# Weight sums by score rows, another order of rooms behind attention, and 640-key rows as 384+256

## The chip, the cores and the metric

The kernel runs on one core of a Trainium2 chip. The metric is device time in microseconds (us) of one launch, as the median of several runs. All numbers of a profile come from one profiled execution.

## The reference

One layer of an encoder on 1024 tokens of width 1024, in float32. It has two token mixers side by side (a causal pooling mixer and a stick-breaking attention of 8 heads), gated and merged, and then a squared-ReLU MLP.

```python
h    = rmsnorm(x, g_pre_mix)
proj = h @ w_in                                   # [u_pool | q | k | v]
y_pool = multiscale_pool(u_pool, ...) @ w_br_pool
# attention, per head, query blocks of 128, causal:
z    = (q @ k.T) * 0.125
attn = sigmoid(z_ts) * prod_{s<j<t} (1 - sigmoid(z_tj)),  s < t
y_sb = (attn @ v) @ w_br_sb
gates  = sigmoid(h @ w_gate + b_gate)             # 2 x 1024 channels
merged = gates[:, :1024] * y_pool + gates[:, 1024:] * y_sb
x = x + rmsnorm(merged @ w_out, g_post_mix)
h2 = rmsnorm(x, g_pre_mlp)
x = x + rmsnorm(square(relu(h2 @ w_up)) @ w_down, g_post_mlp)
```

## The kernel before

Activations lie with channels on the 128 partitions and tokens along the free axis, in two halves of 512 tokens. Every large product is computed from float32 values split into a rounded high part and a low rest (`hi`, `lo`), with three matmuls for one: hi by hi, hi by lo, lo by hi (`mm3`, lines 113 to 117). A product of one 128-row output tile with one half takes 8 steps of 3 matmuls of 512 columns.

The order of instructions on each engine's queue comes from a planner, which simulates the program and issues what it holds ready first; `issue_after(i)` makes what stands in its block follow `i` on the same engine.

**Attention.** For each of the 8 heads, `att_scores` runs over 8 score rows, `i` = 7 down to 0; row `i` holds 128 queries and their (i + 1) x 128 keys. PE computes the scores `z` in pieces of at most 512 keys, from the last key backwards (lines 560 and 563: `q` holds high parts over low rests, so two matmuls are enough). A piece shorter than 256 keys is multiplied at 256 columns. ACT makes `F` and `T` (sigmoids of -z and z, lines 564 and 565), POOL sets the masked part of the last 128 keys of `T` to zero with an affine select (line 567), DVE multiplies `F` up by a scan (line 573) and into `T` (line 577). `att_steps` transposes rows of four (`at`, line 590), ACT and DVE split them into `ahi` and `alo` (598, 599), and PE multiplies them with `v` into `o` (line 615). The sums of `o` go to `oT` (624, 626).

Between these matmuls `pump` puts steps of other products (fillers): later q, k and v, and the gates. A gate's half (`job_gate`) ends with a product on DVE (line 519, tile `gs`), a sigmoid on ACT (520) and a store to DRAM, issued by POOL (521, `gscr`). A change of ACT's table follows the last sigmoid (779).

**Weight sums.** The MLP's down product uses sums of blocks of `w_down`, which are made in DRAM by DMAs alone: `weight_sums` is a generator of 32 DMAs of 1 MB, all issued by POOL (lines 1056 and 1058, destination `wscr`). Sixteen are plain copies and sixteen add to what lies there. The last eight make `s4`: four copies of `s2`, then four additions. They are first read in the down product, far behind attention. Before the change, each store of a gate's half is followed by one.

**Branch products** (`phase_post`). With attention done, ACT and DVE split `oT` into `oh` and `ol` (lines 732 and 733), four tiles each. For every output tile `e` of 8 and both branches `b`, PE computes two halves of 12 matmuls (the pooling branch reads `yh` and `yl`, the attention branch `oh` and `ol`), POOL loads the gate (752), DVE multiplies gate and product (`t`, 756), adds the branches (763) and splits the sum (765), with ACT (764). The first pooling products (`first_pool`) are issued ahead of `phase_post`, and the planner puts those of the second output tile beside them. The products rotate over seven PSUM banks, five of the pool `ps` and two of `dps`.

The tiles of `phase_post` lie in the pool `post`. It takes the room of attention's pools: the tiles `v`, the row tiles `T` and `F` with `ahi` and `alo`, and the small tiles `gs` and `ou`. Each tile waits for the last users of the room it gets (`reuse_waits="tile"`); places are given out in the order in which tags are first asked for. In the same way `ps` takes the banks of attention's `o`, `z` and `at`.

Then follow the output product (`d` from `mg`, first the half h = 0, then h = 1), a chain of norms beside it, and the MLP.

Of the kernel before, what the change touches and what calls it, by code (L numbers as in the profile page):

```python
# [32 lines left out]
P = 128  # L33
# [19 lines left out]
class Block:  # L53
# [460 lines left out]
    def job_gate(self, i, h):  # L514
        nc = self.nc
        d = self.dps.tile([P, H], F32, name="dg", tag="d")
        yield from self.dense_steps(d, self.weights(("g", i)), self.hT[h])
        s = self.sp.tile([P, H], F32, name="gs", tag="gs", bufs=2)
        nc.vector.tensor_mul(s, d, self.rb[h])
        self.after = nc.scalar.activation(s, s, AF.Sigmoid, bias=self.vt[:, V_BG + i : V_BG + i + 1])  # L520
        out = nc.gpsimd.dma_start(self.gscr[i][:, h * H : h * H + H], s)
        with self.tc.issue_after(out.ins):
            next(self.wsums)

    def fillers(self, h):

# [13 lines left out]
    def att_scores(self, h, i):  # L540

        nc = self.nc
        p, j = h // 2, h % 2
        q, qs, k = self.qk[("q", p)][j], self.qk[("qs", p)][j], self.qk[("k", p)][j]
        w = (i + 1) * P
        tl = self.tp.tile([P, w], F32, name="T", tag=f"T{i}", bufs=1)  # L550
        f = self.tp.tile([P, 1024], F32, name="F", tag="F", bufs=1)
        tt = slice(i * P, i * P + P)
        past = self.past[:, 1024 - w :]
        for c in range((w - 1) // H * H, -1, -H):
            n = min(H, w - c)
            top = c + n == w
            cols = slice(c, c + max(256, n))
            z = self.zps.tile([P, H], F32, name="z", tag="z", bufs=3)
            zz = z[:, : max(256, n)]
            m = nc.tensor.matmul(zz, q[:, tt], k[:, cols], start=True, stop=False)  # L560
            if top:
                self.marks.append(m)
            nc.tensor.matmul(zz, qs[:, tt], k[:, cols], start=False, stop=True)  # L563
            nc.scalar.activation(f[:, c : c + n], z[:, :n], AF.Sigmoid, scale=-1.0)  # L564
            nc.scalar.activation(tl[:, c : c + n], z[:, :n], AF.Sigmoid)
            if top:
                nc.gpsimd.affine_select(  # L567
                    out=tl[:, w - P : w], in_=tl[:, w - P : w], pattern=[[-1, P]], compare_op=ALU.is_gt, fill=0.0,
                    base=0, channel_multiplier=1,
                )  # L570

            fr = f[:, c : c + n][:, ::-1]
            nc.vector.tensor_tensor_scan(  # L573
                fr, fr, past[:, c : c + n][:, ::-1], 1.0 if top else f[:, c + n : c + n + 1], ALU.mult, ALU.max
            )
            e = c + n - top
            nc.vector.tensor_mul(tl[:, c:e], tl[:, c:e], f[:, c + 1 : e + 1])  # L577
        return tl
# [66 lines left out]
    def phase_attention(self):  # L645
        tc, nc = self.tc, self.nc
        self.oT = [self.op.tile([P, 1024], F32, name=f"oT{p}", tag=f"oT{p}") for p in range(4)]
        kw = dict(side="right", reuse_waits="tile")
        self.tp = tc.alloc_tile_pool(name="att", bufs=1, **kw)
        self.sp = tc.alloc_tile_pool(name="att_s", bufs=1, **kw)  # L650
        self.credit, self.queue = 0.0, []
        self.w_out = 2.3
        self.pending = None
        self.pin = True
        self.cut = 512
        out = None
        for h in range(8):
            while self.queue:
                self.advance()
            fl = self.fillers(h)  # L660
            n = sum(f[1] for f in fl)
            self.queue = fl
            share = [WS[i] for i in ROWS] if h else [0.0] * 4 + [WS[i] for i in ROWS[4:]]
            w_in = max(0.0, n - (8 if h == 0 else 12) * self.w_out) / sum(share)
            vg = self.job_v(0) if h == 0 else None
            a = {}
            for n_row, i in enumerate(ROWS):
                if n_row == 4:
                    out = self.att_steps(h, 1, [a[r] for r in range(4, 8)])
                a[i] = self.att_scores(h, i)  # L670
                self.pump(w_in * share[n_row])
                if h == 0 and n_row < 4:
                    if n_row == 0:
                        vq = [(vg, 32)] + [(f[0], f[1]) for f in self.fillers(-1)]
                    left = 12 if n_row < 3 else 999
                    while vq and left:
                        left -= 1
                        if next(vq[0][0], self) is self:
                            vq.pop(0)
                if out is not None:  # L680
                    for _ in range(2 if n_row > 3 else 1):
                        next(out, None)
            out = self.att_steps(h, 0, [a[r] for r in range(4)])
        while self.queue:
            self.advance()
        self.queue = self.fillers(8)
        self.w_out = 3.0
        for _ in out:
            pass
        self.pump(self.w_out)  # L690
        self.att_products()
        while self.queue:
            self.advance()
        self.pin = False
        self.cut = 1024
        self.yy = []
        for i in range(8):
            t = self.qp.tile([P, 1024], F32R, name=f"y{'hl'[i % 2]}{i // 2}", tag=("q", "qs", "k")[i % 3], bufs=3)
            nc.gpsimd.dma_start(t.bitcast(F32), self.yscr[i // 2][i % 2].bitcast(F32))
            self.yy.append(t)  # L700
        self.first_pool = [self.dps.tile([P, H], F32, name="dbr", tag="d") for _ in range(2)]
        for h in range(2):
            self.branch_mm(self.first_pool[h], 0, 0, h, (self.yy[0::2], self.yy[1::2]))
        for p in (self.sp, self.tp, self.vp, self.zps):
            p.release()
# [17 lines left out]
    def phase_post(self):  # L723
        tc, nc = self.tc, self.nc
        pp = tc.alloc_tile_pool(name="post", bufs=1, side="right", reuse_waits="tile")
        self.ps = tc.alloc_tile_pool(name="ps", bufs=5, space=PSUM, reuse_waits="tile")
        self.banks = 1
        oh, ol = [], []
        for p in range(4):
            oh.append(pp.tile([P, 1024], F32R, name=f"oh{p}"))  # L730
            ol.append(pp.tile([P, 1024], F32R, name=f"ol{p}"))
            nc.scalar.copy(oh[p], self.oT[p])
            nc.vector.tensor_sub(ol[p], self.oT[p], oh[p].bitcast(F32))
        mg = []
        for h in range(2):
            hi = self.big.tile([P, NK, H], F32R, name=f"mg_hi{h}", tag=f"big_hi{h}")
# [4 lines left out]
        def products(e, b):  # L741
            ds = []
            for h in range(2):
                d = self.bank()
                self.branch_mm(d, e, b, h, xs[b])
                ds.append(d)
            return ds

        def gated(e, b, ds):
            i = 8 * b + e  # L750
            gt = pp.tile([P, 1024], F32, name="gate", tag="gate", bufs=3)
            nc.gpsimd.dma_start(gt, self.gscr[i])
            out = []
            for h in range(2):
                t = pp.tile([P, H], F32, name="t", tag=f"t{b}", bufs=2)
                nc.vector.tensor_mul(t, gt[:, h * H : h * H + H], ds[h])
                out.append(t)
            return out

# [8 lines left out]
        for e in range(8):  # L768
            d0 = nxt
            if e == 0:  # L770
                nxt = products(1, 0)
            p = gated(e, 0, d0)
            d1 = products(e, 1)
            q = gated(e, 1, d1)
            merge(e, p, q)
            if 0 < e < 7:
                nxt = products(e + 1, 0)
        with tc.issue_after(self.after.ins):
            self.table_inst = nc.scalar.preload_act_table_set(TABLES).ins
        pp.release()  # L780
# [9 lines left out]
        for h in range(2):  # L790
# [4 lines left out]
            def mix_out(e, d, first):  # L795
                nc.scalar.copy(mix[e // 4][:, e % 4, :], d)
                sq = acc if first else ch.tile([P, H], F32, name="sq", tag="nf", bufs=2)
                nc.scalar.activation(sq, d, AF.Square)
                if not first:
                    nc.vector.tensor_add(acc, acc, sq)  # L800
# [3 lines left out]
            for e in order:  # L804
                d = self.bank()
                wt = self.weights(("out", 0 if e > 2 else h, e))
                for k, _ in enumerate(self.dense_steps(d, wt, mg[h])):
                    if k == 3 and prev is not None:
                        mix_out(*prev, prev[0] == order[0])
                prev = (e, d)  # L810
            mix_out(*prev, False)
            self.finish_side()
# [550 lines left out]
```

## Time and profile before

| | |
|---|---|
| median of 3 runs | 1279.74 us (1278.86 to 1281.45) |
| profiled execution | 1278.63 us, its span 1276.9 us |
| granted clock of PE | 0.999 |
| PE busy | 1265.7 us, 6035 matmuls |
| DVE busy | 925.7 us |
| ACT busy | 611.0 us |
| POOL busy | 172.1 us |
| DMA | 233.70 MB, of it 88.49 MB on POOL's queue |

PE, PEld (weight loads), DVE, ACT and POOL are engines; SP issues DMAs. In a group's row stand the line, the engine, the operation, the tiles as out<-in, the shapes and the count; after the first bar the busy time in us and the mean duration of one in ns; after the second the idle time of the engine just before these instructions and what ended it. A wait's row has who waited, `<-`, whom for; then us in total, times, the longest. A row of a timeline or of the chain of waits begins with the start in us from the start of the span and the duration in us. "issue" is time in which an engine waited for nothing that the profile shows. In the windows view, the last three columns are PE's granted clock, the busy share of the 16 DMA engines and GB/s.

### The profile page before, as it was taken

To read this page: it belongs to the slowest core of one execution; us is meant where nothing else is said; L and a number is where in the kernel's file an instruction comes from. 1 tells how busy PE (TensorE), PEld (TensorE's weight loads), DVE (VectorE), ACT (ScalarE), POOL (GpSimd) and SP (SyncE) were. 2 spreads that over 40 slices of the span, in tenths; PEclk is the share of its full clock that TensorE was granted. 3 is DMA by queue.
4 is the path that set the end of the run, shared out by engine and by line. 5 is a ranking of instruction groups with operands and counts; after the bars stand their busy time and mean duration, and the time that the engine had idled before them with its cause. 6 is when DMAs were issued, how large, how long until landed. Compare 5 with 4: busy or idle time off the path is not lost.

```text
span 1276.9 us, 16588 instructions
## 1 busy us (share of the span) xinstructions
PE 1265.7 (99%) x6035; PEld 1056.1 (83%) x6035; DVE 925.7 (72%) x1317; ACT 611.0 (48%) x1012; POOL 172.1 (13%) x314
## 2 busy tenths in 40 slices
PE   9999999999999999999999999999999999999997
PEld 6898888889888887888878888888888888888887
DVE  8787688787878737551777979877785655776975
ACT  8235455555555533132456646455454433344452
POOL 1002213211213230000101002211120000001000
PEclk9999999999999999999999999999999999999999
DMA  6254637742757997451529578655569546547651
GB/s 226 66 165 153 210 90 181 147 106 53 185 157 197 248 229 234 142 195 33 179 79 307 181 245 283 216 191 205 177 238 345 194 153 224 191 176 242 200 212 66
DMA packets 75745, 233.70 MB, mean 183 GB/s; under 512 B 8624, under 2 KB 11184, under 8 KB 73488
## 3 DMA queue, kind: packets, MB, share of 16 engines
q1 hardware_dynamic: 47936, 143.64, 34.4%
q0 software_dynamic: 27152, 88.49, 23.1%
q8 instruction: 47, 0.77, 0.2%
q10 hardware_dynamic: 576, 0.52, 0.1%
q14 instruction: 34, 0.28, 0.1%
HBM read 178.10 MB, written 83.89 MB: 205 GB/s over the span
## 4 chain that ended last, share of the span: by engine, by line
PE 91%; DVE 4%; issue 2%; ACT 1%; DMA 1%; POOL 0%; SPq 0%; DVEq 0%; ACTq 0%; POOLq 0%
PE d L116 20%; PE d L117 20%; PE d L115 20%; PE dg L117 4%; PE dg L116 4%; PE dg L113 4%; PE o L615 3%; PE at L590 2%; PE dqk L116 2%; PE dqk L117 2%; PE dqk L113 1%; PE z L563 1%; PE z L560 1%; PE du L116 1%; PE zu L116 1%
## 5 line engine op out<-in xcount | busy, mean ns | idle before, releaser
L116 PE MATMUL d<-blo,whi 128*128 128x512 f32 (+1 forms) x456 | 172.3, 378 | 0.0
L117 PE MATMUL d<-bhi,wlo 128*128 128x512 f32 (+1 forms) x456 | 171.9, 378 | 0.0
L115 PE MATMUL d<-bhi,whi 128*128 128x512 f32 (+1 forms) x456 | 168.7, 378 | 0.0
L573 DVE TENSOR_TENSOR_SCAN F<-F,past 128x512 f32<-128x512 f32 (+3 forms) x96 | 94.0, 979 | 22.4 <-ACT F L564 21.0
L85 ACT CAST whi<-wraw 128x512 fp32r<-128x512 f32 (+1 forms) x88 | 67.7, 800 | 72.4 <-PE d L116 35.0
L113 PE MATMUL dg<-hT_hi,whi 128*128 128x512 f32 x253 | 101.8, 402 | 0.0
L117 PE MATMUL dg<-hT_hi,wlo 128*128 128x512 f32 x256 | 100.8, 394 | 0.0
L116 PE MATMUL dg<-hT_lo,whi 128*128 128x512 f32 x256 | 100.4, 392 | 0.0
L86 DVE TENSOR_TENSOR wlo<-wraw,whi 128x512 fp32r<-128x512 f32 (+1 forms) x88 | 77.6, 904 | 30.1 <-ACT whi L85 30.0
L116 PEld LDWEIGHTS d<-blo,whi 128*128 128x128 f32 x456 | 85.7, 188 | 16.1
L117 PEld LDWEIGHTS d<-bhi,wlo 128*128 128x128 f32 x456 | 85.8, 188 | 15.9
L115 PEld LDWEIGHTS d<-bhi,whi 128*128 128x128 f32 x456 | 85.5, 188 | 15.8
L564 ACT ACTIVATE F<-z 128x512 f32<-128x512 f32 (+3 forms) x96 | 47.2, 493 | 61.6 <-DVE T L577 37.0
L116 PE MATMUL d<-b_lo,whi 128*128 128x512 f32 x196 | 76.2, 390 | 0.4 <-DVE b_lo L825 0.4
L115 PE MATMUL d<-b_hi,whi 128*128 128x512 f32 x196 | 75.6, 389 | 0.0
L117 PE MATMUL d<-b_hi,wlo 128*128 128x512 f32 x196 | 74.7, 389 | 0.0
L1112 DVE TENSOR_TENSOR wlo<-slots_hi,whi 128x1024 fp32r<-128x1024 f32 x29 | 35.5, 1225 | 52.3 <-ACT whi L1110 52.3
L599 DVE TENSOR_TENSOR alo<-at,ahi 128x512 fp32r<-128x512 f32 (+1 forms) x96 | 51.9, 553 | 24.8 <-ACT ahi L598 23.6
L1110 ACT CAST whi<-slots_hi 128x1024 fp32r<-128x1024 f32 x29 | 30.5, 1051 | 81.1 <-PE d L116 65.2
L598 ACT CAST ahi<-at 128x512 fp32r<-128x512 f32 (+1 forms) x96 | 45.1, 481 | 45.2 <-PE at L590 42.0
L1110 ACT CAST whi<-slots_lo 128x1024 fp32r<-128x1024 f32 x27 | 28.4, 1053 | 74.0 <-PE d L116 60.3
L577 DVE TENSOR_TENSOR T<-T,F 128x255 f32<-128x255 f32 (+4 forms) x96 | 52.8, 556 | 12.1 <-POOL T L567 4.2
(319 smaller groups left out, 3310.1 us busy)
## 6 DMA issues: line engine op xcount, KB each, us to landing
wraw<-w SPq DMA_DIRECT2D x80, 512.0 KB, 4.3
wscr<-w POOLq DMA_DIRECT2D x24, 1024.0 KB, 10.3
ext_b<-ascr SPq DMA_DIRECT2D x40, 512.0 KB, 4.3
gscr<-gs POOLq DMA_DIRECT2D x32, 256.0 KB, 4.8
gate<-gscr POOLq DMA_DIRECT2D x16, 512.0 KB, 3.7
pscr<-p SPq DMA_DIRECT2D x32, 256.0 KB, 3.2
braw<-w SPq DMA_DIRECT2D x16, 512.0 KB, 5.5
ascr<-c POOLq DMA_DIRECT2D x32, 256.0 KB, 4.7
```

Of the source, the lines that this page charges most:

```text
L85: nc.scalar.copy(hi[:, c], raw[:, c])
L86: self.last_lo = nc.vector.tensor_sub(lo[:, c], raw[:, c], hi[:, c].bitcast(F32)).ins
L113: nc.tensor.matmul(ps, wh, rh, start=first and i == 0, stop=False)
L115: nc.tensor.matmul(ps, wh, rh, start=first and i == 0, stop=False)
L116: nc.tensor.matmul(ps, wh, rl, start=False, stop=False)
L117: nc.tensor.matmul(ps, wl, rh, start=False, stop=last and i == n - 1)
L564: nc.scalar.activation(f[:, c : c + n], z[:, :n], AF.Sigmoid, scale=-1.0)
L573: nc.vector.tensor_tensor_scan(fr, fr, past[:, c : c + n][:, ::-1], 1.0 if top else f[:, c + n : c + n + 1], ALU.mult, ALU.max)
L577: nc.vector.tensor_mul(tl[:, c:e], tl[:, c:e], f[:, c + 1 : e + 1])
L598: nc.scalar.copy(hi[:, c:], at[:, c:])
L599: nc.vector.tensor_sub(lo[:, c:], at[:, c:], hi[:, c:].bitcast(F32))
L1110: last_split[0] = nc.scalar.copy(hi, src).ins
```

## The change

Six edits:

1. `job_gate` no longer issues a weight sum behind its store.
2. In attention a weight sum is issued on POOL behind the affine select of the score rows number 1, 3 and 6 of each head (rows `i` = 6, 4 and 1): 24 sums. Four more follow the merges of output tiles 1, 3, 5 and 7 in the branch products, and four the output tiles 1, 3, 5 and 7 of the output product's first half.
3. A row's keys are cut in two as 512 below and the rest above, but so that the upper piece has at least 256. Only rows of 640 keys change: 384 below and 256 above in place of 512 and 128.
4. In the pool `post`, the place of the tag `t0` (two tiles of 128x512, 4 KB a partition) is asked for first, ahead of `oh0`.
5. In the pool `ps`, the place of `ms` is asked for first, ahead of the product banks.
6. The products `t` of gate and branch are issued on DVE behind the last `ol`.

```diff
@@ job_gate
-        out = nc.gpsimd.dma_start(self.gscr[i][:, h * H : h * H + H], s)
-        with self.tc.issue_after(out.ins):
-            next(self.wsums)
+        nc.gpsimd.dma_start(self.gscr[i][:, h * H : h * H + H], s)
@@ att_scores
-        for c in range((w - 1) // H * H, -1, -H):
-            n = min(H, w - c)
-            top = c + n == w
+        low = min(H, w - 2 * P) if w > H else 0
+        for c, n in ((low, w - low), (0, low)):
+            if n == 0:
+                continue
+            top = c == low
...
-                nc.gpsimd.affine_select(
+                self.masked = nc.gpsimd.affine_select(
@@ phase_attention
                 self.pump(w_in * share[n_row])
+                if n_row in (1, 3, 6):
+                    with tc.issue_after(self.masked.ins):
+                        next(self.wsums)
@@ phase_post
         self.banks = 1
+        pp.tile([P, H], F32, name="t", tag="t0", bufs=2)
+        self.ps.tile([P, H], F32, name="ms", tag="ms", bufs=1)
...
-            nc.vector.tensor_sub(ol[p], self.oT[p], oh[p].bitcast(F32))
+            ol_done = nc.vector.tensor_sub(ol[p], self.oT[p], oh[p].bitcast(F32)).ins
...
-                nc.vector.tensor_mul(t, gt[:, h * H : h * H + H], ds[h])
+                with tc.issue_after(ol_done):
+                    nc.vector.tensor_mul(t, gt[:, h * H : h * H + H], ds[h])
...
             if 0 < e < 7:
                 nxt = products(e + 1, 0)
+            if e % 2:
+                next(self.wsums)
...
                     if k == 3 and prev is not None:
                         mix_out(*prev, prev[0] == order[0])
+                if h == 0 and e % 2:
+                    next(self.wsums)
```

## The prediction

> **What bounds the kernel now.** I read the page first, then the waits of PE, then the stretches in which PE waits.
>
> ```profile
> PE 1265.7 (99%) x6035; PEld 1056.1 (83%) x6035; DVE 925.7 (72%) x1317; ACT 611.0 (48%) x1012; POOL 172.1 (13%) x314
> ...
> PE 91%; DVE 4%; issue 2%; ACT 1%; DMA 1%; POOL 0%; SPq 0%; DVEq 0%; ACTq 0%; POOLq 0%
> ```
>
> The kernel is a row of matmuls: PE is busy for 99% of the span and carries 91% of the chain that ended last. So only two things can move the time: fewer columns through PE, or fewer places where PE stands. The longest waits of PE inside attention and the branch products are these:
>
> ```profile
> PE d L116 <- DVE ol L733: 0.8, 1, 0.8
> ...
> PE dg L115 <- DVE v L509: 0.4, 1, 0.4
> PE d L115 <- ACT oh L732: 0.3, 1, 0.3
> ```
>
> Those on `ol` and `oh` are one place, the change from attention to the branch products. The timeline of PE shows it (start, duration, instruction):
>
> ```profile
> 483.65 0.39 PE L117 MATMUL d<-yh,wlo 128*128 128x512 f32 x1
> 484.34 0.50 PE L115 MATMUL d<-oh,whi 128*128 128x512 f32 x1 [0.30 <-ACT oh L732]
> 485.60 0.50 PE L116 MATMUL d<-ol,whi 128*128 128x512 f32 x1 [0.76 <-DVE ol L733]
> 485.94 0.39 PE L117 MATMUL d<-oh,wlo 128*128 128x512 f32 x1
> ```
>
> Matmuls overlap, so a wait is read from start to start and not from the idle in brackets. Undisturbed, 12 matmuls of 512 columns take 2.72 us from start to start, 0.227 each:
>
> ```profile
> 518.15 0.39 PE L115 MATMUL d<-yh,whi 128*128 128x512 f32 x1
> ...
> 520.87 0.39 PE L115 MATMUL d<-yh,whi 128*128 128x512 f32 x1
> ```
>
> The three steps here are 0.69, 1.26 and 0.34 us, together 2.29 where 0.68 would do. The place costs 1.6 us. The chain that ended last, over the same place, says why:
>
> ```profile
> 474.94 1.01 DMA gscr<-gs
> 475.95 7.29 issue
> ```
>
> ACT itself is free at 475.95, as its timeline says (474.67 + 1.28), and copies `oh` only at 483.24:
>
> ```profile
> 474.67 1.28 ACT L779 ACT_TABLE_LOAD   x1
> 483.24 3.89 ACT L732 CAST oh<-oT 128x1024 fp32r<-128x1024 f32 x4 [7.29 <-issue]
> ```
>
> The step before, in the chain, is the last gate's store, and its landing is in the DMA view of 474.9 to 475.2 (size, us from issue to landing):
>
> ```profile
> gscr<-gs POOLq DMA_DIRECT2D x1, 256.0 KB, 7.9
> ```
>
> 474.94 + 7.9 = 482.8, then `oh` starts. `oh0` is the first tile of the pool `post`, so this row says that the first place of that pool lies in the room of `gs`, which is free only when the store has read it. The store is slow because POOL's queue and the DMA engines are full: POOL's timeline, and the window of 455 to 490 (the last columns are clock, DMA share, GB/s).
>
> ```profile
> 469.67 1.23 POOL L1056 DMA_DIRECT2D wscr<-w  x1
> 474.94 0.57 POOL L521 DMA_DIRECT2D gscr<-gs  x1 [4.05 <-ACT gs L520]
> 475.93 1.18 POOL L1056 DMA_DIRECT2D wscr<-w  x1 [0.42 <-issue]
> 476.58 2.14 POOL L752 DMA_DIRECT2D gate<-gscr  x3
> ```
>
> ```profile
> 455.00:490.00 35.00, 33.94 (x157) 27.79 (x156) 13.19 (x18) 12.43 (x18) 8.82 (x13) 1.00 1.04 243
> ```
>
> A weight sum stands on either side of the store, and the DMA engines are busy for the whole stretch (1.04).
>
> **Part 1, rows of 640 keys, 384+256 in place of 512+128.** Before, the last 128 keys are multiplied at 256 columns all the same. PE's timeline, the 512 pair of one such row and the next instruction:
>
> ```profile
> 425.81 0.40 PE L560 MATMUL z<-k,q 128*128 128x512 f32 x1
> 426.05 0.40 PE L563 MATMUL z<-k,qs 128*128 128x512 f32 x1
> 426.29 0.40 PE L113 MATMUL dg<-hT_hi,whi 128*128 128x512 f32 x1
> ```
>
> The 256 pair stays and the 512 pair becomes a 384 pair; the kernel has 384 pairs already, in its rows of 896 keys. The other lengths split as before. By groups (after the bar: busy us, mean ns, idle before):
>
> ```profile
> L560 PE MATMUL z<-k,q 128*128 128x512 f32 x48 | 19.2, 399 | 0.0
> ...
> L560 PE MATMUL z<-k,q 128*128 128x384 f32 x16 | 5.5, 342 | 0.0
> ```
>
> 57 ns less for each of 16 matmuls (two a head, 8 heads) is 0.9 us. As a bound, the 512 pair above takes 0.48 from start to start and a pair of 384 this:
>
> ```profile
> 436.48 0.33 PE L560 MATMUL z<-k,q 128*128 128x384 f32 x1
> 436.65 0.34 PE L563 MATMUL z<-k,qs 128*128 128x384 f32 x1
> 436.82 0.40 PE L113 MATMUL dg<-hT_hi,whi 128*128 128x512 f32 x1
> ```
>
> 0.34, so at most 0.14 x 8 = 1.1 us. The lower end is 0.7: where PE waits on DVE, a shorter matmul is eaten by the wait, and one or two heads could lie so. I take 0.9, since PE hardly waits in attention. The sigmoids, scans and products of ACT and DVE touch the same 640 elements in the same number of instructions: nothing.
>
> **Part 2, rooms and order at the branch products.** The first place of `post` goes to `t0`, so `oh0` moves on to a room of attention's row tiles, whose last readers are transposes of the score rows. `oh` can then start when ACT is free, at 475.95 at the latest: `oh0` is done at 477.0 and `ol0` (1.24 on DVE) at 478.3; all four `ol` are done by about 482. PE asks for them from 483.88 on (483.65 + 0.23), so the cover is 5.6 us, and the 1.6 us go. Late next is the gated product: `t` now waits for the gate's store and, by the new order, stands behind the last `ol` on DVE. Behind `t` on DVE wait the merges and the low halves of the next branch weights; PE needs `t` to get a bank back. Before, the first `t` ran here, ended by the landing of the gate load:
>
> ```profile
> 489.42 1.29 DVE L756 TENSOR_TENSOR t<-gate,dbr 128x512 f32<-128x512 f32 x2 [0.47 <-DMA gate<-gscr]
> ```
>
> Seven banks rotate. Two hold the first products, two those of the second output tile, and the products with `oh` start at 483.88; after three halves of 2.72 us all seven are in use, and PE needs the first one back at 492.0. The first `t` is done at 490.1 even if the gate lands as late as now. Cover 1.9 us at worst, more with no sum ahead of the gates. The room held for `ms` moves the product banks to places freed earlier; PE waits for no bank now: nothing. If the cover of `t` were gone, the 1.6 would come back in part; so this term lies between -1.6 and 0, and I take -1.6.
>
> **Part 3, the 32 weight sums.** They are the same DMAs with the same issue cost; 24 now stand behind the masks of rows 6, 4 and 1 of each head, 4 among the branch products, 4 in the first half of the output product. POOL is busy 13% of the span. PE waits for no DMA now, so taking sums from the end of attention gains nothing but what part 2 has counted, and adding them later costs nothing while weights and gates land in time. SP's weight loads share the engines with them: none now comes into the full stretch, and four into the one behind it, where the thirteen gate loads below land in 3.6 us. I take 0, with the ends in the rivals.
>
> **Sum.** -0.9 - 1.6 = -2.5 us. The profiled execution takes 1278.63 us, 1.73 of it outside the span, and becomes 1276.1. It lies 1.1 below the median of the three runs, so on their scale 1279.74 - 2.5 = 1277.2. That is 0.2% of 1279.74 (2.56 us), about what a measurement of this kernel can tell from no change; the forecast sits on that line.
>
> **Rivals.** *One, the place keeps a wait* (the rooms fall otherwise and `oh` still stands on the store, or `t` takes over). For it: the room of `oh0` is only inferred from a wait. Against it: the cover worked out above. Only the columns are left, 1279.7 - 0.9 = 1278.8.
>
> *Two, attention's own two waits go as well,* as the planner lays the work out anew. The longer is the `dg` row above, 0.4 us idle. At `ol` 0.76 idle cost 1.26 - 0.23 = 1.03 from start to start, so 0.4 is about 0.6, and with a smaller wait on `alo` about 1.0, an estimate. For it: DVE's and POOL's queues are ordered anew. Against it: the first waits at the very start of attention, before any sum and any row of 640 keys was issued. 1277.2 - 1.0 = 1276.2.
>
> *Three, slower: the sums hold up the masks.* A sum ahead of a mask in POOL's queue, and DVE just after:
>
> ```profile
> 236.58 1.23 POOL L1056 DMA_DIRECT2D wscr<-w  x1
> 237.26 0.87 POOL L567 TENSOR_SCALAR_AFFINE_SELECT T<-T 128x128 f32<-128x128 f32 x1
> ```
>
> ```profile
> 238.16 0.69 DVE L577 TENSOR_TENSOR T<-T,F 128x511 f32<-128x511 f32 x1 [0.55 <-POOL T L567]
> ```
>
> Behind each of the 24 sums wait the next row's mask, the zero fills of `ahi`/`alo` and the gate stores. At 0.55 us each, passed on to PE, that is 13.2 us and 1290.4. Against it: as many sums stand in that queue now, PE did not wait here, and a sum right behind a mask has the longest time to the next one. It decides from 10 of the 24 on (5.5 us, more than 2.5 + 2.56).
>
> *Four, slower: sums hold up the gate loads.* Both are issued by POOL. Three gates behind a sum landed late, the other thirteen did not (two DMA views, 476.5 to 477.7 and 490 to 548):
>
> ```profile
> gate<-gscr POOLq DMA_DIRECT2D x3, 512.0 KB, 13.5
> ```
>
> ```profile
> gate<-gscr POOLq DMA_DIRECT2D x13, 512.0 KB, 3.6
> ```
>
> A gate is asked for well ahead: this one is for products that PE begins at 518.15 and ends, first half, at 520.87.
>
> ```profile
> 508.45 0.53 POOL L752 DMA_DIRECT2D gate<-gscr  x1 [4.49 <-DVE t L756]
> ```
>
> That is 12.4 us of lead; 13.5 would be 1.1 late, and the bank of that half is needed again only six halves later (16 us). So it decides from a landing of about 28 us, twice the worst seen; four gates late by 1.5 us beyond that would make 1279.7 - 2.5 + 6 = 1283. [...]
>
> **How the numbers follow.** Forecast (both gains) 0.63, own range 1276.2 to 1278.2 for the ends of part 1 and the scatter of a median; rival one 0.15, two 0.10, three 0.08, four 0.04. The forecast lies on the line, so half of it counts as faster (0.32) and half as within 0.2% (0.31). Faster: 0.32 + 0.10 = 0.42. Within: 0.31 + 0.15, and 0.03 of rival three where few sums count, 0.49. Slower: 0.09. The range 1275.0 to 1280.0 holds the forecast and rivals one and two with the runs' scatter of about 1 us; three and four lie above it.
>
> **What the changed profile would show.** Part 1: `z` at 512 columns x40 and at 384 x24. Part 2: no wait of PE on `oh` or `ol`; `oh` of ACT near 476 or earlier, no 7 us before it; `t` after the last `ol`. Part 3: sums at even distances, DMA share of the last 20 us of attention well under 1.0, gates landing in 4 to 14 us without a wait of PE. The prediction is wrong if PE waits on `t`, a gate or a weight in the branch products, if masks hold DVE long enough for a new wait of PE on `alo` or `v`, or if `oh` still stands on a store.

## The result, and the profile after

The changed kernel takes 1303.92 us (median of 5 runs, 1302.48 to 1305.09) against 1279.74 us before: 1.0188 times as long, 95% interval 1.0177 to 1.0200. The forecast was 1277.2 us with a range up to 1280.0; it was wrong, on the side of rival three. The profiled execution takes 1302.48 us with a span of 1300.8 us, 23.9 us more than the span before.

The page's line of engines, and its chain that ended last:

```profile
PE 1272.1 (98%) x6035; PEld 1060.7 (82%) x6035; DVE 925.2 (71%) x1317; ACT 609.7 (47%) x1012; POOL 167.9 (13%) x314
...
PE 86%; DMA 4%; DVE 4%; issue 4%; ACT 1%; POOL 1%; SPq 0%; DVEq 0%; POOLq 0%; ACTq 0%
PE d L116 20%; PE d L117 20%; PE d L115 20%; PE dg L117 3%; PE dg L116 3%; PE dg L113 3%; DMA wscr<-w 3%; PE o L616 2%; PE dqk L116 2%; PE dqk L117 2%; PE at L591 2%; PE dqk L113 1%; PE z L564 1%; PE z L561 1%; DVE F L574 1%
```

PE stands for 1300.8 - 1272.1 = 28.7 us where it stood 11.2 before: +17.5. It is also busy for 6.4 us more, with the same 6035 matmuls. Together that is the 23.9. And a weight sum (`wscr<-w`) has come into the chain.

Where it lies is read from two starts, of the first `dbr` (in an answer on that tile: shortest, median and longest in ns, first and last start) and of the first product with `mg`. Before:

```profile
L115 PE MATMUL dbr<-yh,whi x8: 389/389/389, 473.0 to 480.3; 128*128 128x512 f32 x8
```

```profile
561.67 0.39 PE L115 MATMUL d<-mg_hi,whi 128*128 128x512 f32 x1
```

After:

```profile
L115 PE MATMUL dbr<-yh,whi x8: 389/389/389, 498.5 to 505.8; 128*128 128x512 f32 x8
```

```profile
585.54 0.39 PE L115 MATMUL d<-mg_hi,whi 128*128 128x512 f32 x1
```

Attention ends 25.5 us later. The branch products take 87.0 us where they took 88.7, which is 1.6 us less. From `mg` on nothing changes: 1300.8 - 585.5 is 215.3 and 1276.9 - 561.7 is 215.2. So all of the loss lies in attention, and the waits of PE in its last hundred us name it:

```profile
PE o L616 <- POOL ahi L597: 11.8, 2, 8.7
PE o L616 <- ACT ahi L599: 4.2, 2, 3.8
PE o L616 <- DVE alo L600: 1.9, 1, 1.9
```

Line 597 is a zero fill of `ahi` on POOL, some 0.2 us of work. What POOL itself waited for in that stretch:

```profile
POOL wscr L1070 <- DMA wscr<-w: 38.1, 4, 11.4
POOL wscr L1068 <- DMA wscr<-wscr: 16.2, 3, 6.5
```

Line 1070 issues a copy and line 1068 an addition. POOL stood 54 us in front of weight sums, each time for the landing of another sum. POOL's timeline shows the last case (issue or work, and in brackets the idle time ahead of it):

```profile
463.55 1.72 POOL L1068 DMA_DIRECT2D wscr<-w  x1
466.25 0.61 POOL L521 DMA_DIRECT2D gscr<-gs  x1 [0.98 <-ACT gs L520]
...
468.07 0.30 POOL L568 TENSOR_SCALAR_AFFINE_SELECT T<-T 128x128 f32<-128x128 f32 x1
479.44 0.51 POOL L1070 DMA_DIRECT2D wscr<-wscr  x1 [11.06 <-DMA wscr<-w]
479.93 0.22 POOL L597 MEMSET ahi<- 128x128 f32 x1
```

and PE's timeline what it cost:

```profile
470.93 0.60 PE L591 MATMUL at<-eye,T 128*128 128x128 f32 x4
480.21 0.58 PE L616 MATMUL o<-ahi,v 128*128 128x256 f32 x1 [8.68 <-POOL ahi L597]
480.59 0.63 PE L113 MATMUL dg<-hT_hi,whi 128*128 128x512 f32 x1
481.02 0.63 PE L116 MATMUL dg<-hT_lo,whi 128*128 128x512 f32 x1
```

The addition into a block of `s2` is issued at 463.55. The copy of that same block into `s4` follows it, reads what the addition writes, and so is held at the head of POOL's queue until the addition has landed, 16 us after its issue. The zero fill behind it comes at 479.93 and PE's next `o` at 480.21.

The other two kinds of waits, on `ahi` of ACT and `alo` of DVE, reach PE through the masks, which stand in the same queue. DVE's product of a row waits for its mask:

```profile
DVE T L578 <- POOL T L568: 26.6, 6, 7.1
```

Before, these waits of DVE were 1.4 us over the same stretch of attention, and in the kernel *e1* below, which ties the eight last sums, 0.8. Behind the product, DVE and ACT are late for the next `ahi` and `alo`: the mask held by the copy at 456.54 comes at 457.07, DVE's product at 457.41 and PE's wait on `alo` ends at 458.62.

The eight last sums, these copies into `s4` and the additions behind them, are not where the program puts them. Its text has the copies in the branch products and the additions in the output product, but these eight are the only ones without an `issue_after`; the planner issues first what it holds ready, and it moved all eight up, each close behind the sum that it depends on. That its simulation let these sums land sooner than the chip does is inferred from this order, not seen. In the order of the program three other sums lie between a sum and the one that needs it; in the order issued, none does. Before the change these eight sums were issued at attention's end as well, but in their order: a copy 27 to 31 us behind the addition that it reads, and POOL waited for no landing.

The matmuls behind the wait are slow as well. Their starts lie 0.43 us apart, not 0.227. After the four longest waits (8.9, 4.0, 3.4 and 2.1 us from start to start, less the usual step) 7, 7, 7 and 4 matmuls of 512 columns run like this; 25 times 0.20 is 5 us, most of the 6.4 that PE is busier. The four waits give 18.3 us, the slow matmuls 5.0, smaller waits the rest of attention's 25.5.

Both, the wait of POOL and the slow matmuls of PE, stand in the trace. POOL stands idle for 11.06 us ahead of the copy at 479.44, until the landing of `wscr<-w`. PE's granted clock (windows view) is 1.00 from 470 to 472, 0.50 from 480 to 482, where the starts lie 0.43 us apart, and 1.00 again from 484 to 486. On the idle time ahead of slow matmuls see the last section.

The other two parts did what the prediction said. `z`, by groups and shapes (lines 561 and 564, of which the first is shown):

```profile
L561 PE MATMUL z<-k,q 128*128 128x512 f32 x40 | 16.1, 402 | 0.0
...
L561 PE MATMUL z<-k,q 128*128 128x384 f32 x24 | 8.3, 344 | 0.0
```

ACT and DVE at the branch products (timelines):

```profile
500.17 1.28 ACT L789 ACT_TABLE_LOAD   x1
501.47 3.90 ACT L739 CAST oh<-oT 128x1024 fp32r<-128x1024 f32 x4
```

```profile
502.55 4.63 DVE L740 TENSOR_TENSOR ol<-oT,oh 128x1024 fp32r<-128x1024 f32 x4 [1.76 <-ACT oh L739]
507.10 1.28 DVE L764 TENSOR_TENSOR t<-gate,dbr 128x512 f32<-128x512 f32 x2
```

`oh` starts as soon as the table is loaded, where it had stood 7.29 us; `t` follows the last `ol`; PE has no wait in the branch products.

### The profile page after: what moved, and what is told of

Read it like the earlier page. It is cut to its first block, busy times and chain, and to the rows that moved or that the text cites. A ratio compares the mean times of both kernels' runs of the same rounds, so it can differ in the third digit from the quotient of the medians.

```text
span 1300.8 us, 16593 instructions
## 1 busy us (share of the span) xinstructions
PE 1272.1 (98%) x6035; PEld 1060.7 (82%) x6035; DVE 925.2 (71%) x1317; ACT 609.7 (47%) x1012; POOL 167.9 (13%) x314
## 4 chain that ended last, share of the span: by engine, by line
PE 86%; DMA 4%; DVE 4%; issue 4%; ACT 1%; POOL 1%; SPq 0%; DVEq 0%; POOLq 0%; ACTq 0%
PE d L116 20%; PE d L117 20%; PE d L115 20%; PE dg L117 3%; PE dg L116 3%; PE dg L113 3%; DMA wscr<-w 3%; PE o L616 2%; PE dqk L116 2%; PE dqk L117 2%; PE at L591 2%; PE dqk L113 1%; PE z L564 1%; PE z L561 1%; DVE F L574 1%
## 5 line engine op out<-in xcount | busy, mean ns | idle before, releaser
L574 DVE TENSOR_TENSOR_SCAN F<-F,past 128x256 f32<-128x256 f32 (+2 forms) x96 | 94.1, 980 | 19.1 <-ACT F L565 18.0
L565 ACT ACTIVATE F<-z 128x256 f32<-128x256 f32 (+2 forms) x96 | 47.2, 493 | 71.0 <-DVE T L578 51.7
L578 DVE TENSOR_TENSOR T<-T,F 128x255 f32<-128x255 f32 (+3 forms) x96 | 53.1, 556 | 36.1 <-POOL T L568 28.1
```

Of the source, the lines that this page charges most:

```text
L574: nc.vector.tensor_tensor_scan(fr, fr, past[:, c : c + n][:, ::-1], 1.0 if top else f[:, c + n : c + n + 1], ALU.mult, ALU.max)
```

## The experiments

"Before" is run again beside each set; its medians are 1278.9 to 1279.3 us. All ratios are to it, with 95% intervals in brackets; they are not quotients of the medians, and differ from these by up to 0.0009.

**Which part carries the loss.** *e1_anchored*: the changed kernel, with the eight last sums tied to gate loads.

```diff
-            nc.gpsimd.dma_start(gt, self.gscr[i])
+            self.gate_dma = nc.gpsimd.dma_start(gt, self.gscr[i]).ins
...
             if e % 2:
-                next(self.wsums)
+                with tc.issue_after(self.gate_dma):
+                    next(self.wsums)
# the same for the four in the output product
```

> The changed kernel, but the last eight weight sums are held behind gate loads on POOL, so the planner cannot issue them inside attention; the other 24 stay behind the masks. Theory (the loss comes from the last eight, which the planner issued at attention's end, where each waits for the landing of the sum issued just before it and holds up POOL's queue): the loss goes and the two gains stay, about 1277.2 us (1276 to 1278.5), no wait of PE over 0.7 us in attention. Rival masks (24 sums behind masks hold up the row work): as the changed kernel, about 1303. Rival load (too many bytes in flight at attention's end): in between, 1280 to 1295, since six sums still lie there.

Measured: 1276.59 us, 0.9985 (0.9976 to 0.9994), span 1274.8. Attention's end by windows (busy us and instructions of PE, PEld, DVE, ACT, POOL; PE's clock; DMA share; GB/s), first the changed kernel, then e1:

```profile
390.00:470.00 80.00, 70.26 (x325) 57.09 (x324) 46.89 (x77) 33.80 (x75) 22.42 (x39) 0.94 0.77 192
```

```profile
390.00:470.00 80.00, 79.60 (x402) 66.65 (x401) 53.52 (x88) 40.40 (x86) 21.05 (x40) 1.00 0.62 165
```

Only the place of the eight sums differs, and it is worth 26 us by the spans and 27 by the medians.

*e3_sums_only*: the kernel before, with only edits 1 and 2 of the change (no rows, rooms or order).

> The kernel before with the edits to the weight sums alone: rows and rooms as before. If the sums carry the whole loss: the changed kernel's time plus the two gains it lacks, 1304 to 1307 us. If rooms or rows carry it: about 1280.

Measured: 1301.38 us, 1.0179 (1.0165 to 1.0193), 2.6 us under the least expected. The edits to the sums alone lose 22.5 us, so rooms and rows are not needed for the loss.

The expectation was also wrong in one point: e3 lacks only one of the two gains. Its branch products take 87.0 us, as in the changed kernel, though `oh` still stands on the last gate's store (ACT waits 4.42 us for its landing, until 504.17). With fewer sums around it the store lands before PE asks for `oh` at 507.45. So moving the sums gains the 1.6 us of part 2 by itself, and so do the rooms (e5 below).

**What in the eight sums costs it: the bytes, the masks, or the waits.** *e7_no_wait*: nearly as many bytes in attention's end, one sum behind each of seven masks in heads 6 and 7, but none that needs a recent one.

```diff
-                if n_row in (1, 3, 6):
+                if n_row in ((1, 3, 6) if h < 6 else range(7)):
...
-            (False, s2, s3), (True, s2, (1, 1)), (False, s4, s2), (True, s4, (0, 1)),
+            (False, s2, s3), (True, s2, (1, 1)), (False, s4, (0, 1)), (True, s1, (0, 1)),
# and none in the branch products or the output product
```

> The changed kernel with seven sums in each of heads 6 and 7, one behind each of seven masks, and three a head before; none after attention. The last eight are made so that none has to wait for a sum issued shortly before: four copy w_down's block (0,1) where the copies of s2 should stand, and four add that block to s1 in place of s4, so s1 and s4 are not the sums that the down product needs. Fourteen sums of 1 MB lie in the last two heads, as in the changed kernel, and none waits. Theory: no block of POOL, 1277 to 1280 us. Rival load: as the changed kernel, 1295 to 1305. Rival masks: at least 1303.

Measured: 1278.62 us, 0.9995 (0.9986 to 1.0004). Its window, and its sums between 390 and 495 (size, median us from issue to landing):

```profile
390.00:470.00 80.00, 79.25 (x398) 65.92 (x397) 52.75 (x88) 39.67 (x86) 25.46 (x47) 1.00 0.98 258
```

```profile
wscr<-w POOLq DMA_DIRECT2D x11, 1024.0 KB, 12.4
```

The DMA engines are fuller than in the changed kernel (0.98 against 0.77), the sums land no sooner (12.4 us against 10.9), one stands behind each of seven masks of a head, and PE loses next to nothing. Neither the load by itself nor a mask's place behind a sum is the cause. A sum that waits for nothing does not hold POOL's queue for long: in the kernel before, the eleven sums that POOL issues between 406 and 477 took it 0.51 to 1.26 us each (POOL's timeline).

*e8_tiny_waits*: e1, with four small DMAs on POOL (2 KB each) behind the next masks, each reading a block that the sum just before adds to.

```diff
+                        q = self.n_sums - 20
+                        self.n_sums += 1
+                        if q >= 0:
+                            self.nc.gpsimd.dma_start(self.tiny[q], self.wscr[1][q][0:1, 0, :])
```

> The kernel with the last eight sums held behind gate loads, plus four DMAs of 2 KB which read what sums 21 to 24 write, so each waits on POOL's queue for the landing of a sum just issued; no load is added. Theory: four waits like the four of 38.1 us in all that the changed kernel has before its copies, so some two thirds of its loss comes back: 1294 us (1288 to 1300), with waits of PE on ahi or alo of several us. Rival load and rival masks: nothing added, the same as the kernel without the four.

Measured: 1276.87 us, 0.9977 (0.9967 to 0.9987). This missed: the wait theory as it stood gave 1294. POOL does wait (waits, then one of them in POOL's timeline), and PE does not:

```profile
POOL tiny L681 <- DMA wscr<-w: 18.0, 3, 7.3
```

```profile
408.75 0.51 POOL L681 DMA_DIRECT2D tiny<-wscr  x1 [7.28 <-DMA wscr<-w]
```

So a wait of POOL is not passed on one for one; a single one of 7 us is absorbed here. The theory had to be narrowed: either two waits in a row or longer ones are needed. Three kernels tell these apart. *e9_copies_early*: as changed, but only the four additions tied to gate loads, so the four copies are moved up. *e10_two_waits*: e9, and a 2 KB DMA in the place of each addition, which waits for the copy.

```diff
# e10, beside e9's tie in the output product
+                nc.gpsimd.dma_start(self.tiny[e // 2], self.wscr[3][e // 2][0:1, 0, :])
```

*e11_bytes_no_second_wait*: four copies moved up, and behind each a 1 MB addition to a block that was finished long before, so the bytes without the second wait.

```diff
+                with tc.issue_after(self.last_sum):
+                    nc.gpsimd.dma_start(self.wscr[0][e // 2], self.dn_w(0, 1, e // 2), accum_op=ALU.add)
# and none in the output product
```

> The changed kernel with the four copies of s2 left as in it (the planner issues them at attention's end, each just behind the sum it waits for), and the four additions to s4 held behind the last gate load. Four single waits of POOL, with 4 MB of copies. The four tiny DMAs showed single waits of 7 us without a wait of PE. Theory single wait covered: no or little loss, 1277 to 1280 us. Theory load counts as well: with 4 MB more in flight a landing takes over 8 us, and 2 to 8 us come back, 1279 to 1285.

> As the kernel with the four copies early, and behind each copy, in the place in POOL's queue where the changed kernel has the addition to s4, a DMA of 2 KB that waits for that copy's landing; the additions are held behind the last gate load. Theory two waits in a row (POOL blocked for 13 us and more, beyond what PE's lead covers): half or more of the loss of 24 us comes back, 1288 to 1300 us. Theory load (the additions' 4 MB are what makes it slow): like the kernel with copies alone.

> The changed kernel with the four last additions made to s1 in place of s4, each issued right behind its copy: the same bytes at the same place in POOL's queue, but the addition need not wait for the copy just issued (s1 and s4 are not the sums that the down product needs). With the copies alone 1278.9, with copies and a second wait but not the bytes 1287.8, with both about 1303. Theory: the second wait is the larger part and the bytes lengthen what is left of it, so 1281 to 1290 us. Theory load: the additions' bytes alone make the rest, 1295 to 1303.

| | POOL's waits for landings at attention's end | median, us | ratio |
|---|---|---|---|
| e9, one wait | 25.2 us in 4, longest 7.5 | 1278.86 | 1.0000 (0.9990 to 1.0010) |
| e10, two waits, few bytes | 25.1 in 4 and 18.7 in 4 | 1287.84 | 1.0066 (1.0050 to 1.0082) |
| e11, one wait, all bytes | 32.2 in 4, longest 11.4 | 1293.88 | 1.0105 (1.0089 to 1.0122) |
| changed kernel, both | 38.1 in 4 and 16.2 in 3 | 1303.92 | 1.0188 (1.0177 to 1.0200) |

e10 came out just under what was expected and e11 above it. The waits of POOL in e9, e10 and e11:

```profile
POOL wscr L1071 <- DMA wscr<-w: 25.2, 4, 7.5
```

```profile
POOL wscr L1073 <- DMA wscr<-w: 25.1, 4, 7.0
POOL tiny L789 <- DMA wscr<-wscr: 18.7, 4, 6.8
```

```profile
POOL wscr L1070 <- DMA wscr<-w: 32.2, 4, 11.4
```

In e10 the first pair stands at 408 and 416, POOL's timeline:

```profile
408.54 0.51 POOL L1073 DMA_DIRECT2D wscr<-wscr  x1 [7.02 <-DMA wscr<-w]
409.04 0.59 POOL L522 DMA_DIRECT2D gscr<-gs  x1
416.33 0.50 POOL L789 DMA_DIRECT2D tiny<-wscr  x1 [6.71 <-DMA wscr<-wscr]
416.82 0.22 POOL L598 MEMSET ahi<- 128x128 f32 x1
```

The first wait is e8's at 408.75, which cost nothing. The second follows it with one gate store between, and PE stands from 414.6 to 417.1 for `ahi`. In e11 PE stands behind the longest single wait (PE's timeline):

```profile
473.68 0.58 PE L616 MATMUL o<-ahi,v 128*128 128x256 f32 x1 [7.08 <-POOL ahi L597]
```

That one is a wait of 11.45 us, until 471.27. So both count: by the medians the second wait alone costs 9 us (e10 against e9), the bytes alone 15 (e11 against e9), and together they cost the changed kernel's 25; with intervals of about 2 us on each, that the two add up is not shown closely. The profiled executions of e10 and e9 lie only 3.8 us apart, as e10's is the fastest of its four runs and e9's one of the slower of its ten. The bytes lengthen the waits of the copies: the last two of the four are 10.3 and 11.4 us in e11 and 7.1 and 5.9 in e9. This is not all that they do. In e11 DVE also stands 6.1 us, until 423.97, for the landing of a gate's store before it can write the next `gs`, and PE then waits 0.5 and 1.6 us; the changed kernel has no such wait. PE's lead over POOL covers most single waits of up to 7 us here; what goes beyond reaches PE, with slow matmuls on top (in e11 those behind the wait that ends at 473.68 start 0.43 us apart). The lead is not the same everywhere: e9, with one wait of 4.7 to 7.5 us for each copy, has two waits of PE (2.2 and 0.6 us in its profiled execution, which is 2.4 us above its median), and its median lies some 2 us above e1's.

**The other parts, each alone.** *e4_rows*: the kernel before with edit 3 alone. *e5_rooms*: with edits 4 to 6 alone. *e2_rows_rooms*: with edits 3 to 6, the sums behind the gate stores as before. Their diffs are the hunks of the change.

> The kernel before with rows of 640 keys as 384 + 256 and nothing else. As predicted for this part: 0.9 us less (0.7 to 1.1), ratio 0.9993; the span near 1276.0.

> The kernel before with the rooms for t0 and ms and the products t behind the last ol, and nothing else; the sums still crowd attention's end. As predicted for this part: 1.6 us less, ratio 0.9987, and no wait of PE on oh or ol though the last gate's store lands as late as before. If the crowd of sums was what held oh, nothing is gained.

> The kernel before with the new rows and the new rooms, the sums behind the gate stores as before: what the prediction's sum holds, without the moved sums. Predicted 2.5 us less than before, ratio 0.998; by the profiles of the single parts 1.9 to 2.2 us less, ratio 0.9984.

Measured: e4 1278.66 us, 0.9999 (0.9990 to 1.0008); e5 1277.40, 0.9984 (0.9975 to 0.9992); e2 1276.49, 0.9974 (0.9964 to 0.9984). In e5 PE runs through the change to `oh` at its full step:

```profile
483.65 0.39 PE L117 MATMUL d<-yh,wlo 128*128 128x512 f32 x1
483.88 0.39 PE L115 MATMUL d<-oh,whi 128*128 128x512 f32 x1
484.11 0.39 PE L116 MATMUL d<-ol,whi 128*128 128x512 f32 x1
```

and its branch products take 87.0 us, 1.6 less, as in the changed kernel. In e4 the time from the first `dg` to the first `dbr` is 365.9 us against 366.5 before, 0.6 less; its profiled execution loses 1.6 us ahead of attention, where no row of 640 keys has yet run, and takes 1.0 less in the branch products, though no room has changed: PE comes later to `oh`, whose store lands no later. So its median says nothing on 0.6. Why the start differs was not found; the first `dg` begins between 106.3 and 108.1 in the kernels here.

*e6_four_a_head*: the changed kernel with all 32 sums behind masks, rows number 1, 3, 5 and 6, none later. *e12_old_rows*: e1 with the rows cut as before.

> The changed kernel with four sums a head, behind the masks of the score rows number 1, 3, 5 and 6, and none after attention; nothing is left for the planner to move. A copy of s2 stands a whole head behind the sum that it reads. Theory: no wait of POOL on a landing, as the kernel with the last eight held, 1276 to 1278 us. Rival masks: a third more sums behind masks than there, 1280 or more.

> The kernel with the last eight sums held behind gate loads, with rows of 640 keys as before (512 + 128). If the columns are worth what was predicted, 0.9 us slower than with the new rows, 1277.5 us; the profiles of the two show that attention loses a part of it to waits, so 0.3 to 0.6 us slower.

Measured: e6 1276.74 us, 0.9978 (0.9967 to 0.9988), with no wait of POOL on a sum; 32 sums behind 32 masks are harmless here, where each copy stands a whole head behind its source. e12 1278.88 us, 0.9988 (0.9979 to 0.9997); its profiled execution takes 2.5 us more than e1's, of which 1.5 lie ahead of attention and 1.0 in it (367.1 against 366.1 from the first `dg` to the first `dbr`). The rows are worth 0.6 to 1.0 by these two pairs.

e1, e2, e5, e6 and e8 beat both kernels, at 0.9974 to 0.9985; their intervals overlap, so no best one can be named. Of these, e6 is the simplest mend of the change, and e2 is the change without its edits to the sums.

## Why the prediction was wrong

**What bounds the kernel, and the sum of parts 1 and 2: right.** PE is the bound, and with the sums out of the way both gains come: forecast -2.5 us, measured -2.3 (e1) and -2.9 (e2) by the medians. That it fits so closely is in part luck: by the ratios these are -1.9 and -3.3, and the starts of attention alone scatter by 1.8 us. Part 2 was right in its mechanism and its size (-1.6 predicted, 1.6 in e5 and in the changed kernel), and `oh0` did stand in the gate store's room. What it missed is that the moved sums alone take the wait away as well (e3), so either half of the change is enough for the same 1.6 us. Part 1 is right in its counts; its size was taken as 0.9, and the traces give 0.6 (e4) and 1.0 (e1 against e12). The bound below it, "where PE waits on DVE, a shorter matmul is eaten by the wait", fits e4: the changed kernel and e1 have two new waits of PE on DVE of some 0.6 us in attention, e4 has the first of them in full, and e12, with the old rows, has neither. That they take from the gain is likely, and no run holds them apart.

**Part 3: the step that failed.** It reads "24 now stand behind the masks of rows 6, 4 and 1 of each head, 4 among the branch products, 4 in the first half of the output product", and takes 0 since "adding them later costs nothing". The last eight were not added later. The places were read off the program, while the text ahead of the prediction says that the planner issues what it holds ready first unless `issue_after` ties it. The diff ties 24 of 32 sums; the eight without a tie were the thing to ask about: where will they go, and what do they need? The answer lies in the list of sums: copies of `s2`, then additions to `s4`, each on the landing of one four places ahead. In place of that 0 the runs show POOL held 54 us for landings, PE late on `ahi` and `alo` through zero fills and masks, and 26 to 27 us lost. The rows at hand could have given a price: the profile's page has a median of 10.3 us from issue to landing for the sums that read `w`, and POOL's timeline has sums, masks and zero fills in one row, so a sum that is moved up to its source can hold POOL for some 10 us.

**Rival three: the right direction, the wrong sums and the wrong price.** It had POOL's queue holding up masks and zero fills and PE paying for it. But it charged 0.55 us of issuing to the 24 sums behind masks, which cost next to nothing (attention is 0.3 us longer in e6 than in e2), and nothing to the eight others, which cost 25 us by waiting. Its 1290.4 and its turning point of 10 sums have no support in the runs.

**Rivals one, two and four** did not come: PE has no wait in the branch products, on `oh`, `t` or a gate, and of attention's own two waits the longer stayed (0.37 us).

**Signs given for the change.** Of those that would make it wrong, "if masks hold DVE long enough for a new wait of PE on `alo` or `v`" came true (1.9 us on `alo`); the "sums at even distances" did not come.

## What to carry to other kernels

In these kernels a DMA on POOL that depended on one issued just ahead of it stood at the head of POOL's queue until that one had landed (waits of 4.8 to 11.4 us at the changed kernel's attention end, and up to 16 us from issue to landing), and what stood behind it on POOL came after it; so leave at least the time of a landing between the two, or issue it where nothing urgent stands behind. Where a planner orders the queues, what a diff leaves untied has no place of its own: list it, and ask of each what it needs and how far up it can go. Before pricing a wait, ask how much lead the bound engine has over the waiting one: here a wait below it was free (7.3 us in e8), and above it the bound engine stood (7.1 us, behind a wait of 11.4, in e11).

## What the runs showed of the hardware

PE's clock after a wait. The changed kernel's 8.7 us of idle time are followed by 3.0 us (480.2 to 483.2) at a granted clock of 0.50. Two idle times of 2.5 us, equal within 0.01, ended differently. PE's timeline in e10:

```profile
417.10 0.38 PE L617 MATMUL o<-ahi,v 128*128 128x256 f32 x1 [2.50 <-POOL ahi L598]
...
417.87 0.63 PE L565 MATMUL z<-k,qs 128*128 128x512 f32 x1
418.30 0.63 PE L113 MATMUL dg<-hT_hi,whi 128*128 128x512 f32 x1
```

and in e3:

```profile
418.11 0.39 PE L613 MATMUL o<-ahi,v 128*128 128x256 f32 x1 [2.51 <-POOL ahi L594]
...
418.72 0.40 PE L561 MATMUL z<-k,qs 128*128 128x512 f32 x1
418.95 0.39 PE L113 MATMUL dg<-hT_hi,whi 128*128 128x512 f32 x1
```

Eight matmuls of 512 columns started 0.40 to 0.43 us apart in the one and none in the other (0.22 to 0.24 there), which makes the same wait 1.6 us dearer. After the changed kernel's wait of 1.90 us on `alo`, four ran so. So slow matmuls came after idle times of 1.90 and 2.50 us and did not come after one of 2.51; what decides it, no run here shows.
